# Two transformer blocks on one core: 64-row score products widened to 128 rows with zeros, and weight low parts moved from GpSimd to VectorE

## The chip, the cores and the metric

The kernel runs on one core of a Trainium2 chip. A core has five engines with instruction streams of their own: TensorE (PE; its weight loads are listed as PEld), VectorE (DVE), ScalarE (ACT), GpSimd (POOL) and SyncE (SP, which only issues transfers here). The metric is device time in microseconds; smaller is better.

## The reference, cut to what matters

A sequence of 512 tokens with 1024 features passes through four layers, all in float32: a latent attention (mla), a differential attention (diff), a convolution and pooling mixer, and a forgetting attention with a convolution. Each is followed by a layer norm, a SwiGLU feed-forward network (FFN) with 2816 hidden features and another layer norm. What the change touches:

```
# mla: 8 heads; a query and a key have a part of 128 features and a rotated part of 64
logits = einsum('bqhd,bkhd->bhqk', qn_b, k_nope) + einsum('bqhd,bkd->bhqk', qr_b, k_rope)
# diff: 8 heads with two maps (m) of 64 features each
logits = einsum('bqhmd,bkhmd->bmhqk', q_b, k) * scale - slopes * dist
p = softmax(where(chunk_mask, logits, NEG_BIG));  a = p[:, 0] - lam * p[:, 1]
# FFN
gate, up = split(x @ w_gu, 2);  y = (silu(gate) * up) @ w_down
```

## The kernel before, in words

**Precision.** A factor of a product is held as two float32r tiles, a high part (ScalarE copies, line 170 for weights) and a low part (the difference, line 171). `mm3` (lines 371 to 373) adds three products: high by high, low by high, high by low. A weight tile of 128x1024 is loaded by SP into `wraw` (2 buffers) and split into `whi` and `wlo` (5 buffers each). The tuple `ONPOOL` names the weights whose low part GpSimd makes; a list of exceptions turns single tiles around, none of them a `down` tile. The FFN's `win` tiles (gate and up together, combined by the sums of lines 193 to 198 as for a Strassen product) are always split by VectorE. Each of the four FFNs has 22 `down` tiles, the weights of its second product: 88 in all.

**First attention (mla).** Heads are worked in a pipeline: `scores(h + 1)`, `head(h + 2)`, `attend(h)`. A block of scores takes `mm3` over the 128 features, then line 981, where `sq` holds the rotated query's high part in rows 0 to 63 and its low part in rows 64 to 127 and `kk` holds the key's high part twice, and then line 982, the query's high part by the key's low part, over 64 rows only. There are 8 heads of 4 blocks, 128 to 512 columns wide.

**Second attention (diff).** The same pipeline. `stack` (line 1080) lays a query map's high and low part into the two halves of one 128-row tile, the other map the other way round, and duplicates the key's high part. Both maps' key low parts share one tile `kl`: map 0 in rows 0 to 63, map 1 in rows 64 to 127, with two buffers. A block is line 1164 (128 rows) and line 1166 (64 rows: high part of the query by `kl`), for each of two maps. The softmax is a VectorE reduction with a bias (line 1036), an exponential on ScalarE (1037) and, for diff, a combination of both maps on VectorE (1187); the result is transposed on PE (1052), split again (1065, 1067) and multiplied by the values in `attend`.

**Order.** Outside a few stretches written out by hand (in `project_out`), a scheduler in the build sets the order on every engine from the order of the code, the tiles' buffers and its own costs. At run time each engine works in that order and waits on semaphores. PSUM has four `acc`, two `ps` and two `tr` banks.

Of the kernel before, what the change touches and what calls it, by code (L numbers as in the profile page):

```python
# [10 lines left out]
F32R = mybir.dt.float32r  # L11
# [5 lines left out]
P = 128  # L17
S = 512
# [32 lines left out]

LNS = [(i, k) for s in ("", "_2") for i in range(2) for k in ("ln_mix_#" + s, "ln_ffn_#" + s)]

ONPOOL = ("od_x", "od_v", "od_q", "od_k", "od_o", "uq_n", "ukv", "df_o", "mla_o", "down")
OTHERWISE = (11, 12, 15, 20, 23, 24, 25, 73, 79, 80, 81, 82, 83, 84, 85, 86, 88, 90, 91, 100, 102, 103, 224, 226, 231)
NORM_ACT = (1, 3, 6, 7, 12, 13, 16, 24, 25, 26, 30)
ROPE_POOL = (1, 2, 3, 4, 5, 7, 9, 11)
# [18 lines left out]
HALF = (slice(0, 64), slice(64, 128))  # L76
# [66 lines left out]
class Weights:  # L143
# [30 lines left out]
    def steps(self):  # L174
# [7 lines left out]
        if name != "win":  # L182
            on_pool = (name in ONPOOL) != (self.at - 1 in OTHERWISE)
            self.ready.append((name, *self.split((self.hi, self.lo), raw[0], 0, n, nc.gpsimd if on_pool else nc.vector)))
# [129 lines left out]
def kernel(ctx: ExitStack, tc: tile.TileContext, a: dict, out: bass.AP):  # L314
    nc = tc.nc

    def f32(ap):
        return ap.bitcast(F32)
# [17 lines left out]
    def acc():  # L336
        return bank("acc")
# [496 lines left out]
    def mla(xT, close_x, open_x, names):  # L834
        with pool("mla_o") as op_:
            cmask = op_.tile([P, S], F32, name="cmask")
            with ExitStack() as st:
# [34 lines left out]
                for part, (key, n) in enumerate((("mla_a", 384), ("mla_b", 320))):  # L872
                    ps = [bank() for bank in ((acc,) * 4, (pss, pss, acc, acc))[part]]
# [11 lines left out]
                    for t in range(NT):  # L885
                        sq = ip.tile([P, 384], BF16, name="sq", tag="sq", bufs=2)
                        i = part * 4 + t
# [13 lines left out]
                kk = ap_.tile([P, S], F32R, name="kk")  # L901
                kkl = ap_.tile([P, S], F32R, name="kkl")

                QR = {}
                for u in range(2):
                    wh, wl = W.next("uq_r", 3, 256)
                    qr = ip.tile([P, NT, 4, 2, 64], F32, name="qr")
                    for t in range(NT):
                        ps = acc()
                        ts = slice(t * P, (t + 1) * P)  # L910
                        for k in range(3):
                            mm3(ps[:, :256], cqh[:, k, ts], cql[:, k, ts], wh[:, k], wl[:, k], k == 0, k == 2)
                        rope_on(qr[:, t], ps[:, :256].rearrange("p (h d) -> p h d", d=64), t, 4)
                    if u == 0:
                        for j in range(2):
                            turn_c(3 + j, ckh[:, j], ckl[:, j])
                        ps = pst()
                        for t in range(NT):
                            nc.tensor.transpose(ps[:, t * P:(t + 1) * P], kr[:, t].rearrange("p a b d -> p (a b d)"), ident)
                        nc.scalar.activation(kk, ps, AF.Copy)  # L920
                        nc.vector.tensor_sub(kkl[0:64], ps[0:64], f32(kk[0:64]))
                    for h in range(4):
                        ps = pst()
                        for t in range(NT):
                            nc.tensor.transpose(ps[:, t * P:(t + 1) * P], qr[:, t, h].rearrange("p a d -> p (a d)"), ident)
                        QR[4 * u + h] = sq = ap_.tile([P, S], F32R, name="sq_r", tag="sq_r", bufs=8)
                        nc.scalar.activation(sq, ps, AF.Copy, scale=-MLA_SCALE)
                        nc.vector.scalar_tensor_tensor(sq[64:128], ps[64:128], -MLA_SCALE, f32(sq[64:128]),
                                                       op0=OP.mult, op1=OP.subtract)
# [3 lines left out]
                Q, V, O = {}, {}, {}  # L933
# [37 lines left out]
                def scores(h):  # L971
                    qh, ql, kh, kl = Q.pop(h)
                    sq = QR.pop(h)
                    PT[h] = pt = Pt(cp, 2)
                    todo = []
                    for qb in range(NT):
                        n = (qb + 1) * P
                        qs = slice(qb * P, n)
                        ps = pss()
                        mm3(ps[:, :n], qh[:, qs], ql[:, qs], kh[:, :n], kl[:, :n], True, False)  # L980
                        nc.tensor.matmul(ps[:, :n], sq[:, qs], kk[:, :n], start=False, stop=False)
                        nc.tensor.matmul(ps[:, :n], sq[0:64, qs], kkl[0:64, :n], start=False, stop=True)
                        mark("mla", f"s{h}.{qb}")
                        e = cp.tile([P, S], F32, name="e", tag="e", bufs=2)
                        sums = small.tile([P, 4], F32, name="sums", tag="sums", bufs=6)
                        softmax(e, ps, n, cmask[:, S - n:], sums[:, 0:1], sums[:, 1:2])
                        todo.append((qb, n, e, sums))
                        if len(todo) > LAG:
                            rest(h, pt, *todo.pop(0))
                    while todo:  # L990
                        rest(h, pt, *todo.pop(0))
# [85 lines left out]
                mm3(ps[:, kb * P:], vh[kb], vl[kb], self.t[g, "h"][:, kb % 2, o:], self.t[g, "l"][:, kb % 2, o:],  # L1077
                    kb == 0, kb == NT - 1)

    def stack(p, ps, s, scale, i):  # L1080


        hi = [p.tile([P, S], F32R, name="qh", tag=f"qh{s}{m}", bufs=2) for m in range(2)]
        lo = [hi[m][HALF[1 - m]] for m in range(2)]
        if s:
            kl = p.tile([P, S], F32R, name="kl", tag="kl", bufs=2)
            lo = [kl[HALF[m]] for m in range(2)]
        for m in range(2):
            nc.scalar.activation(hi[m][HALF[m]], ps[HALF[m]], AF.Copy, scale=1.0 if s else scale)
        for m in range(2):  # L1090
            h = f32(hi[m][HALF[m]])
            if s:
                nc.vector.tensor_sub(lo[m], ps[HALF[m]], h)
                if i in DUP_ACT:
                    nc.scalar.activation(hi[m][HALF[1 - m]], h, AF.Copy)
                else:
                    nc.gpsimd.tensor_copy(hi[m][HALF[1 - m]], h)
            else:
                nc.vector.scalar_tensor_tensor(lo[m], ps[HALF[m]], scale, h, op0=OP.mult, op1=OP.subtract)
        return hi + [kl] if s else hi  # L1100

    def diff(xT, close_x, open_x, FIRST, names):
        with pool("df_o") as op_:
            st = ExitStack()
            dp = st.enter_context(pool("diff"))
# [14 lines left out]
            nc.vector.tensor_scalar(lam[:, 6:7], par("g_sub", 0), 1.0 - LAMBDA_INIT, None, op0=OP.mult)  # L1120
            nlam, gsub = lam[:, 5:6], lam[:, 6:7]
            xh, xl = xT
            Q, V, O = {}, {}, {}

            def values(p):
# [14 lines left out]
            def head(h):  # L1140
                got = []
                for s in range(2):
                    if h < 2:
                        ps = FIRST[2 * h + s]
                    else:
                        ps = acc()
                        project_T(ps, W.next(("df_q", "df_k")[s], KD, P), xT, KD)

                    got += stack(dp, ps, s, -0.125 * 2.0 ** (h + 1), h)
                Q[h] = got  # L1150

            PT, S0 = {}, {}

            def scores(h):
                q0, q1, k0, k1, kl = Q.pop(h)
                PT[h] = pt = Pt(dp, 2) if h < 7 else Pt(lp, 1)
                S0[h] = s0 = small.tile([P, 3, NT], F32, name="s0", tag="s0", bufs=3)
                todo = []
                for qb in range(NT):
                    n = (qb + 1) * P  # L1160
                    qs = slice(qb * P, n)
                    pm = [pss() for m in range(2)]
                    for m, (q, k) in enumerate(((q0, k0), (q1, k1))):
                        nc.tensor.matmul(pm[m][:, :n], q[:, qs], k[:, :n], start=True, stop=False)
                    for m, q in enumerate((q0, q1)):
                        nc.tensor.matmul(pm[m][:, :n], q[HALF[m], qs], kl[HALF[m], :n], start=False, stop=True)
                    mark("df", f"s{h}.{qb}")
                    sums = small.tile([P, 8], F32, name="sums8", tag="sums8", bufs=4)
                    e = []
                    for m in range(2):  # L1170
                        e.append(dp.tile([P, S], F32, name=f"e{m}", tag=f"e{m}", bufs=2))
                        softmax(e[m], pm[m], n, dist[:, S - n:], sums[:, m:m + 1],
                                s0[:, 0, qb:qb + 1] if m == 0 else sums[:, 2:3], 2.0 ** -(h + 1))
                    todo.append((qb, n, e, sums))
                    if len(todo) > LAG:
                        rest(pt, s0, *todo.pop(0))
                while todo:
                    rest(pt, s0, *todo.pop(0))
                nc.vector.reciprocal(s0[:, 1], s0[:, 0])
                nc.vector.tensor_mul(s0[:, 2], s0[:, 1], s0[:, 1])  # L1180
# [32 lines left out]
            def normalise(h, ps, ss):  # L1213
# [9 lines left out]
                O[h] = oh, ol  # L1223

            head(0)
            head(1)
            scores(0)
            values(0)
            late = None
            for h in range(8):  # L1230
# [544 lines left out]
    f = None  # L1775
    for step in steps:
        xT, f = step(xT, f)
# [108 lines left out]
```

## Time and profile before

| | |
|---|---|
| median of 3 runs | 2301.66 us (2300.28 to 2306.31) |
| the profiled execution | 2304.18 us, its span 2302.4 us |
| PE busy | 2250.3 us (98%), 14148 products |
| DVE busy | 1770.4 us (77%) |
| ACT busy | 997.1 us (43%) |
| POOL busy | 471.3 us (20%), 280 instructions |
| granted PE clock, mean | 0.989 |

The first attention's scores run from 64 to 173 us of the span and the second's from 588 to 792 us; the four FFNs lie around 200 to 560, 800 to 1190, 1300 to 1680 and 1910 to 2290 us. In the rows below a product's end is modelled and products overlap in the pipeline, so the distance from the start of one product to the start of the next is what it costs; the busy share alone does not show it.

### The profile page before, as it was taken

The page shows a single profiled execution, that of the slowest core. Times are in us where ns is not written, and L with a number is a line of the kernel's source. Part 1 is how long each engine was busy: PE and PEld are TensorE (multiplying, and loading weights), DVE is VectorE, ACT ScalarE, POOL GpSimd, SP SyncE. Part 2 cuts the span into 40 slices and gives each one's busy share as a digit, 9 for nine tenths or more (in the row PEclk, how much of TensorE's full clock was granted, in tenths as well). Part 3 has the DMA queues.
Part 4 walks back from the last instruction along what each step waited for, and adds up shares of the span by engine and source line. Part 5 has one row for each costly group of instructions (what it writes and reads, how often), then busy time and mean ns, then how long its engine had stood idle before and what let it go on. Part 6 is the DMA issues. An engine that isn't in the chain of part 4 may idle for free. (4 is left out here: it accounts for less than half of the span.)

```text
span 2302.4 us, 35345 instructions
## 1 busy us (share of the span) xinstructions
PE 2250.3 (98%) x14148; PEld 1988.6 (86%) x14148; DVE 1770.4 (77%) x2718; ACT 997.1 (43%) x1665; POOL 471.3 (20%) x280
## 2 busy tenths in 40 slices
PE   8999999999999999999999999999998999999997
PEld 8878999998888789999988899999886768999996
DVE  5667888886656688888765588888767766988886
ACT  4654444333555554443333244434334654444341
POOL 2200111113321111111210011111246531111112
PEclk9999999999999999999999999999998989999999
DMA  5112233332222033333233233332232112233321
GB/s 180 55 45 92 92 106 105 111 92 90 92 66 73 28 110 101 102 110 109 86 106 100 64 129 110 110 101 92 83 96 74 37 37 101 92 110 110 101 92 65
DMA packets 59365, 210.51 MB, mean 91 GB/s; under 512 B 6624, under 2 KB 6880, under 8 KB 59200
## 3 DMA queue, kind: packets, MB, share of 16 engines
q1 hardware_dynamic: 56304, 198.97, 27.5%
q0 software_dynamic: 2320, 8.23, 1.1%
q8 instruction: 111, 1.82, 0.3%
q10 hardware_dynamic: 576, 1.05, 0.1%
q14 instruction: 54, 0.44, 0.1%
HBM read 206.12 MB, written 2.10 MB: 90 GB/s over the span
## 5 line engine op out<-in xcount | busy, mean ns | idle before, releaser
L170 ACT ACTIVATE whi<-wraw 128x1024 fp32r<-128x1024 f32 (+3 forms) x528 | 521.0, 989 | 831.0 <-PE acc L372 301.3
L171 POOL TENSOR_TENSOR wlo<-wraw,whi 128x1024 fp32r<-128x1024 f32 (+2 forms) x141 | 355.8, 2526 | 1281.4 <-ACT whi L170 1030.2
L171 DVE TENSOR_TENSOR wlo<-wraw,whi 128x1024 fp32r<-128x1024 f32 (+3 forms) x387 | 429.3, 1110 | 136.8 <-ACT whi L170 136.1
L371 PE MATMUL acc<-xh,whi 128*128 128x256 f32 (+1 forms) x1712 | 527.3, 308 | 0.0
L372 PE MATMUL acc<-xl,whi 128*128 128x256 f32 (+1 forms) x1712 | 524.2, 306 | 3.1 <-DVE xl L481 3.1
L373 PE MATMUL acc<-xh,wlo 128*128 128x256 f32 (+1 forms) x1712 | 522.8, 305 | 3.1 <-DVE wlo L171 3.1
L372 PEld LDWEIGHTS acc<-xl,whi 128*128 128x128 f32 x1712 | 322.9, 189 | 28.5 <-DVE xl L481 4.3
L371 PEld LDWEIGHTS acc<-xh,whi 128*128 128x128 f32 x1712 | 322.9, 189 | 24.8 <-issue 0.9
L373 PE MATMUL acc<-xs,wlo 128*128 128x256 f32 x1216 | 342.6, 282 | 0.0
L372 PE MATMUL acc<-xql,whi 128*128 128x256 f32 x1216 | 341.4, 281 | 0.0
L371 PE MATMUL acc<-xs,whi 128*128 128x256 f32 x1216 | 340.0, 280 | 0.4 <-ACT sums L768 0.4
L373 PEld LDWEIGHTS acc<-xh,wlo 128*128 128x128 f32 x1712 | 322.9, 189 | 20.0 <-DVE wlo L171 4.1
L371 PEld LDWEIGHTS acc<-xs,whi 128*128 128x128 f32 x1216 | 229.9, 189 | 4.4 <-ACT sums L768 0.8
L372 PEld LDWEIGHTS acc<-xql,whi 128*128 128x128 f32 x1216 | 228.5, 188 | 5.7
L373 PEld LDWEIGHTS acc<-xs,wlo 128*128 128x128 f32 x1216 | 228.4, 188 | 0.0
L371 PE MATMUL tr<-whi,hh 128*128 128x512 f32 (+1 forms) x296 | 118.1, 399 | 0.0
L372 PE MATMUL tr<-wlo,hh 128*128 128x512 f32 (+1 forms) x296 | 116.9, 395 | 0.0
L373 PE MATMUL tr<-whi,hl 128*128 128x512 f32 (+1 forms) x296 | 115.8, 391 | 0.0
L373 PE MATMUL ps<-whi,hl 128*128 128x512 f32 x288 | 113.7, 395 | 0.0
L371 PE MATMUL ps<-whi,hh 128*128 128x512 f32 x288 | 113.2, 393 | 0.0
L372 PE MATMUL ps<-wlo,hh 128*128 128x512 f32 x288 | 113.2, 393 | 0.0
L431 DVE SCALAR_TENSOR_TENSOR res<-res,acc 128x512 f32<-128x512 f32 x87 | 58.9, 683 | 55.2 <-PE acc L373 54.9
(353 smaller groups left out, 4195.6 us busy)
## 6 DMA issues: line engine op xcount, KB each, us to landing
wraw<-in_gu_dram SPq DMA_DIRECT2D x176, 512.0 KB, 3.7
wraw<-in_dn_dram SPq DMA_DIRECT2D x88, 512.0 KB, 3.4
wraw<-in_ev_in_dram SPq DMA_DIRECT2D x16, 512.0 KB, 3.5
wraw<-in_mla_o_dram SPq DMA_DIRECT2D x8, 512.0 KB, 3.5
wraw<-in_df_q_dram SPq DMA_DIRECT2D x8, 512.0 KB, 3.4
wraw<-in_df_k_dram SPq DMA_DIRECT2D x8, 512.0 KB, 3.5
wraw<-in_df_v_dram SPq DMA_DIRECT2D x8, 512.0 KB, 3.4
wraw<-in_df_o_dram SPq DMA_DIRECT2D x8, 512.0 KB, 3.4
```

Of the source, the lines that this page charges most:

```text
L170: self.nc.scalar.activation(hi, raw[:, o:o + n], AF.Copy)
L171: eng.tensor_sub(lo, raw[:, o:o + n], hi.bitcast(F32))
L371: nc.tensor.matmul(ps, ah, bh, start=first, stop=False)
L372: nc.tensor.matmul(ps, ah, bl, start=False, stop=False)
L373: nc.tensor.matmul(ps, al, bh, start=False, stop=last)
L431: nc.vector.scalar_tensor_tensor(y, y, ALPHA if first else 1.0, ps, op0=OP.mult, op1=OP.add, accum_out=SUMS[t][:, c:c + 1] if sums else None)
```

## The change

Three edits. The key's low parts get tiles of their own, 128 rows high with zeros in the half that belongs to the other operand, and lines 982 and 1166 multiply over all 128 rows. In the second attention these are two tiles (`kl0`, `kl1`), made once for all heads, instead of one tile with two buffers; `scores(0)` now stands ahead of `head(1)`. And `down` leaves `ONPOOL`: its 88 low parts are made by VectorE.

```diff
-ONPOOL = ("od_x", "od_v", "od_q", "od_k", "od_o", "uq_n", "ukv", "df_o", "mla_o", "down")
+ONPOOL = ("od_x", "od_v", "od_q", "od_k", "od_o", "uq_n", "ukv", "df_o", "mla_o")
...
-                        nc.vector.tensor_sub(kkl[0:64], ps[0:64], f32(kk[0:64]))
+                        nc.vector.tensor_sub(kkl[HALF[0]], ps[HALF[0]], f32(kk[HALF[0]]))
+                        nc.gpsimd.memset(f32(kkl[HALF[1]]), 0.0)
...
-                        nc.tensor.matmul(ps[:, :n], sq[0:64, qs], kkl[0:64, :n], start=False, stop=True)
+                        nc.tensor.matmul(ps[:, :n], sq[:, qs], kkl[:, :n], start=False, stop=True)
...
-    def stack(p, ps, s, scale, i):
+    def keys_low(p):
+        kl = [p.tile([P, S], F32R, name=f"kl{m}") for m in range(2)]
+        for m in range(2):
+            nc.gpsimd.memset(f32(kl[m][HALF[1 - m]]), 0.0)
+        return kl
+
+    def stack(p, ps, s, scale, i, low=None):
...
-        lo = [hi[m][HALF[1 - m]] for m in range(2)]
-        if s:
-            kl = p.tile([P, S], F32R, name="kl", tag="kl", bufs=2)
-            lo = [kl[HALF[m]] for m in range(2)]
+        lo = [low[m][HALF[m]] if s else hi[m][HALF[1 - m]] for m in range(2)]
...
-                    for m, (q, k) in enumerate(((q0, k0), (q1, k1))):
+                    for m, (q, k, l) in enumerate(((q0, k0, l0), (q1, k1, l1))):
                         nc.tensor.matmul(pm[m][:, :n], q[:, qs], k[:, :n], start=True, stop=False)
-                    for m, q in enumerate((q0, q1)):
-                        nc.tensor.matmul(pm[m][:, :n], q[HALF[m], qs], kl[HALF[m], :n], start=False, stop=True)
+                        nc.tensor.matmul(pm[m][:, :n], q[:, qs], l[:, :n], start=False, stop=True)
...
             head(0)
+            scores(0)
             head(1)
-            scores(0)
             values(0)
```

Where instructions stand now. On PE, in the second attention, head 5's last score block (`ps_7500`, 512 columns) was followed by products of a projection (`acc_7916`) and head 6's first block (`ps_7787`), whose key low part has a buffer of its own (`kl_7616` beside `kl_7399`):

```order
L1164 MATMUL ps_7500<-qh_7397,qh_7360 128x512
L1166 MATMUL ps_7500<-kl_7399,qh_7360 128x512
L372 MATMUL acc_7916<-xl_5623,whi_7635 128x512
L373 MATMUL acc_7916<-xh_5622,wlo_7636 128x512
L1052 MATMUL tr_7516<-ident_76,e0_7474 128x128 x2
L371 MATMUL acc_7916<-xh_5622,whi_7635 128x512
L372 MATMUL acc_7916<-xl_5623,whi_7635 128x512
L373 MATMUL acc_7916<-xh_5622,wlo_7636 128x512
L1164 MATMUL ps_7787<-qh_7614,qh_7577 128x128
L1166 MATMUL ps_7787<-kl_7616,qh_7577 128x128
```

Now the same place reads so (`ps_7500` and `ps_7499` are head 5's last block, `ps_7785` head 6's first):

```order
L1170 MATMUL ps_7500<-qh_7398,qh_7361 128x512
L1171 MATMUL ps_7500<-kl1_6114,qh_7361 128x512
L1170 MATMUL ps_7499<-qh_7397,qh_7360 128x512
L1171 MATMUL ps_7499<-kl0_6113,qh_7360 128x512
L1053 MATMUL tr_7515<-ident_76,e0_7473 128x128 x2
L1170 MATMUL ps_7785<-qh_7613,qh_7576 128x128
L1171 MATMUL ps_7785<-kl0_6113,qh_7576 128x128
L371 MATMUL acc_7914<-xh_5623,whi_7633 128x512
```

Both heads use the one tile `kl0_6113`, with two transposes and one product between the last use by head 5 and the first by head 6; the projection's products stand behind. On DVE at that place, the write of the key low parts for head 6 (line 1098, 1093 before) now stands between the softmax reductions (line 1037) of the two maps of head 5's last block, and waits for PE:

```order
L1037 ISA e1_7509,sums8_7505<-ps_7500,dist_6101 128x512 [waits DVE_49,PE_49]
L1190 TENSOR_SCALAR sums8_7485<-sums8_7485,s0_7452,lam_6103 128x1 [waits DVE_49,Activation_49]
L1098 TENSOR_TENSOR kl0_6113<-acc_7582,qh_7613 64x512 [waits PE_49]
L1098 TENSOR_TENSOR kl1_6114<-acc_7582,qh_7614 64x512
L1037 ISA e0_7506,sums8_7505<-ps_7499,dist_6101 128x512 [waits PE_49]
L1104 SCALAR_TENSOR_TENSOR qh_7908<-acc_7877,qh_7908 64x512 [waits Activation_49]
```

Before, the same two writes (into `kl_7616`) stood about 45 instructions earlier on DVE and waited for ScalarE alone. In the first FFN, POOL's queue held one row of 23 low parts, 22 of them `down` tiles; now the one that is left is the next stage's:

```order
L419 DMA lnb<-in_ln_ffn_b_dram 128x1024
L171 TENSOR_TENSOR wlo<-wraw,whi 128x1024
L389 TENSOR_TENSOR lnr<-lnv,mhalf 128x1 x3
```

The 22 stand on DVE, among the sums of the `win` tiles (lines 193 to 198) and the additions that empty PSUM (771 to 782, 431). One hidden unit of the first FFN now, on DVE; the first row is a `down` tile:

```order
L171 TENSOR_TENSOR wlo<-wraw,whi 128x1024
L774 TENSOR_TENSOR sums<-sums,acc 128x256
L194 TENSOR_TENSOR wraw<-wraw 128x512
L777 TENSOR_TENSOR sums<-sums,acc 128x2x256
L431 SCALAR_TENSOR_TENSOR res_80<-res_80,ps 128x512
L197 TENSOR_TENSOR wraw<-wraw 128x512
L171 TENSOR_TENSOR wlo<-wraw,whi 128x1024
L198 TENSOR_TENSOR wraw<-wraw 128x512
L782 TENSOR_TENSOR sums<-sums,acc 128x512
```

## Rows read from the trace of the kernel before

**Rows 1.** The page's first part: busy us, share, instructions.

```profile
PE 2250.3 (98%) x14148; PEld 1988.6 (86%) x14148; DVE 1770.4 (77%) x2718; ACT 997.1 (43%) x1665; POOL 471.3 (20%) x280
```

**Rows 2.** Attention stretches: window, PE, PEld, DVE, ACT, POOL busy, PEclk, DMA, GB/s.

```profile
60.00:180.00 120.00, 118.61 (x630) 94.87 (x629) 78.90 (x218) 66.71 (x165) 16.33 (x8) 1.00 0.15 46
588.00:812.00 224.00, 220.32 (x1181) 176.14 (x1179) 139.86 (x383) 121.75 (x323) 50.23 (x31) 0.99 0.21 64
```

**Rows 3.** Sum over four FFN stretches: 260:540, 860:1140, 1350:1640, 1960:2240.

```profile
sum 1130.00, PE 1129.63 PEld 1048.02 DVE 971.77 ACT 457.81 POOL 193.99; mean PE 282.41 PEld 262.00 DVE 242.94 ACT 114.45 POOL 48.50
```

**Rows 4.** Lines 1166 and 982: count, ns min/median/max, starts, forms.

```profile
L1166 PE MATMUL ps<-kl,qh x64: 323/410/501, 588.8 to 791.8; 64*128 64x128 f32 x16, 64*128 64x256 f32 x16, 64*128 64x384 f32 x16, 64*128 64x512 f32 x16
L982 PE MATMUL ps<-kkl,sq_r x32: 323/410/502, 64.5 to 173.1; 64*128 64x128 f32 x8, 64*128 64x256 f32 x8, 64*128 64x384 f32 x8, 64*128 64x512 f32 x8
```

**Rows 5.** PE's timeline, a 512-column score block: start, us, line, tile.

```profile
685.41 0.39 PE L371 MATMUL acc<-xh,whi 128*128 128x512 f32 x1
685.64 0.39 PE L1164 MATMUL ps<-qh 128*128 128x512 f32 x1
685.95 0.50 PE L1166 MATMUL ps<-kl,qh 64*128 64x512 f32 x1
686.38 0.50 PE L372 MATMUL acc<-xl,whi 128*128 128x512 f32 x1
686.72 0.39 PE L373 MATMUL acc<-xh,wlo 128*128 128x512 f32 x1
```

**Rows 6.** PE's timeline, a 128-column score block behind products of values.

```profile
636.00 0.22 PE L371 MATMUL ps<-pth,vh 128*128 128x128 f32 x1
636.06 0.28 PE L372 MATMUL ps<-ptl,vh 128*128 128x128 f32 x1
636.18 0.27 PE L373 MATMUL ps<-pth,vl 128*128 128x128 f32 x1
636.29 0.28 PE L1164 MATMUL ps<-qh 128*128 128x128 f32 x1
636.49 0.32 PE L1166 MATMUL ps<-kl,qh 64*128 64x128 f32 x1
636.74 0.50 PE L371 MATMUL acc<-xh,whi 128*128 128x512 f32 x1
637.08 0.40 PE L372 MATMUL acc<-xl,whi 128*128 128x512 f32 x1
```

**Rows 7.** PE's timeline, two 64-row products side by side.

```profile
588.57 0.33 PE L1164 MATMUL ps<-qh 128*128 128x128 f32 x2
588.83 0.33 PE L1166 MATMUL ps<-kl,qh 64*128 64x128 f32 x2
589.09 0.38 PE L371 MATMUL acc<-whi,xh 128*128 128x256 f32 x1
589.31 0.28 PE L372 MATMUL acc<-wlo,xh 128*128 128x256 f32 x1
```

**Rows 8.** PE's waits: who waited for whom, total us, times, longest.

```profile
PE tr L1052 <- DVE e L1187: 1.6, 1, 1.6
PE ps L371 <- DVE sums L1036: 1.3, 2, 0.9
```

**Rows 9.** DVE by line and form: count | busy us, mean ns | idle before.

```profile
L171 DVE TENSOR_TENSOR wlo<-wraw,whi 128x1024 fp32r<-128x1024 f32 x299 | 366.3, 1225 | 114.4 <-ACT whi L170 114.2
L194 DVE TENSOR_TENSOR wraw<-wraw 128x512 f32<-128x512 f32 x76 | 99.8, 1313 | 0.0
L198 DVE TENSOR_TENSOR wraw<-wraw 128x512 f32<-128x512 f32 x76 | 91.8, 1207 | 0.1
L777 DVE TENSOR_TENSOR sums<-sums,acc 128x512 f32<-128x512 f32 x76 | 52.2, 687 | 3.8 <-PE acc L373 1.2
```

**Rows 10.** POOL's and DVE's timelines in the last FFN, at one `down` tile.

```profile
2241.44 2.54 POOL L171 TENSOR_TENSOR wlo<-wraw,whi 128x1024 fp32r<-128x1024 f32 x1 [13.11 <-ACT whi L170]
...
2241.75 2.79 DVE L197 TENSOR_TENSOR wraw<-wraw 128x512 f32<-128x512 f32 x1
```

More of the change, by code (lines that the diff above doesn't have):

```diff
@@ L1099, in stack @@
                 nc.vector.scalar_tensor_tensor(lo[m], ps[HALF[m]], scale, h, op0=OP.mult, op1=OP.subtract)
-        return hi + [kl] if s else hi
+        return hi + low if s else hi
     def diff(xT, close_x, open_x, FIRST, names):
@@ L1122, in diff @@
             xh, xl = xT
+            KL = keys_low(dp)
             Q, V, O = {}, {}, {}
@@ L1147, in head @@
                         project_T(ps, W.next(("df_q", "df_k")[s], KD, P), xT, KD)
-                    got += stack(dp, ps, s, -0.125 * 2.0 ** (h + 1), h)
+                    got += stack(dp, ps, s, -0.125 * 2.0 ** (h + 1), h, KL)
                 Q[h] = got
@@ L1154, in scores @@
             def scores(h):
-                q0, q1, k0, k1, kl = Q.pop(h)
+                q0, q1, k0, k1, l0, l1 = Q.pop(h)
                 PT[h] = pt = Pt(dp, 2) if h < 7 else Pt(lp, 1)
```

## The prediction

> **What bounds the kernel now.** The first view is the page's table of engines [rows 1]: PE is busy 98% of the span, the next one, DVE, 77%. That share alone says little, since the stages have different limits and a product's end is modelled. So the second view is the table of stretches. Over the four FFNs PE is busy 1129.63 of 1130 us, DVE 971.77 [rows 3]; in the first attention PE 118.61 of 120 and DVE 78.90, in the second 220.32 of 224 and 139.86 [rows 2]. PE sets the pace wherever the change reaches, at full granted clock (1.00, 1.00 and 0.99 in those rows), and an edit is worth what it takes out of PE's own sequence, less what PE then waits. The third view is PE's timeline, read from start to start [rows 5 to 7]: there the reader sees what the busy share hides, products that follow each other at a steady distance, and a stumble at each 64-row product.
>
> **The change part by part.** *64 rows to 128.* In a stream a 512-column product takes 0.23 us (685.41 to 685.64) and a 128-column one 0.06 (636.00 to 636.06). At the 512-column block the distances are 0.31 from line 1164 to the 64-row product, 0.43 from there to the next and 0.34 to the one after: 1.08 for three products that cost 3 x 0.23 = 0.69 in a stream, 0.39 more [rows 5]. At the 128-column block they are 0.20, 0.25 and 0.34: 0.79, where the stream takes 0.06 + 0.06 + 0.23 = 0.35, 0.44 more [rows 6]. That a group of sums ends there is not the reason: the 128-row product at 636.18 ends one too, and its successor follows after 0.11. So a 64-row product among 128-row ones costs about 0.39 us on top of its columns, at entry and at exit, and over 128 rows, zeros or not, it should cost the stream's distance. There are 32 in the first attention and 64 in the second, with the same durations in both [rows 4]. The first: 32 x 0.39 = 12.5. In the second, two pairs stand side by side; such a pair takes 0.74 from 588.57 to 589.31 with the product behind it, against 4 x 0.06 + 0.12 = 0.36 in a stream (256 columns at half of 512's), so 0.38 for two [rows 7]; 60 x 0.39 + 2 x 0.38 = 24.2. Together 36.7 us off PE. The bounds for this term are 0 (a 128-row product with zeros stumbles as well) and 36.7; I take the upper one, since the rows of 128-row products around it show no stumble anywhere.
>
> Rows 7 also show the other side: two products in different halves of the array run at the same time, one 0.33 us for both. Widened, they no longer can. The Trainium skill has both rules on one page (TensorEngine Tiling (Array Packing), Key Properties): changing the tiling mode drains the array, which speaks for the change, and different tiles execute in parallel, which speaks against it. By the second rule alone 32 products, one of each pair, were free before and would now be paid.
>
> *Zeros.* Three memsets go to POOL, which is busy 16.33 of 120 and 50.23 of 224 us in these stretches [rows 2]: nothing, and if POOL's idle time did not cover them, three of its mean instruction, 471.3 / 280 = 1.7, so 5 us [rows 1].
>
> *One pair of key tiles instead of two buffers.* At each of seven changes of head DVE's write of the new low part now waits for the last low product of the head before, and PE's first low product of the new head waits for DVE. The way round is that product, 0.50 (its own duration, row 685.95 of [rows 5]), and a 512-column DVE operation, 0.69 (nearest: line 777 in [rows 9]): 1.19, less what PE has in between. By the order, the early heads have a row of projection products there and the last changes little: two transposes and one product between heads 5 and 6. I take 1 us at each of the last three changes, 3 us; the bounds are 0 and 7 x 1.19 = 8.3. Behind the waiting write on DVE stand the reduction of the other map's block and the new head's query parts, and ScalarE's exponential waits for the first of these. The moved `scores(0)` costs nothing: PE has the 96 value products of 256 columns (96 x 0.12 = 11.5 us) to lay beside it.
>
> *The softmax behind a faster PE.* Scores go through DVE and ScalarE before PE turns them and multiplies by the values; those take as long as before, and PE now comes sooner, by 4 x 0.39 = 1.6 us a head in the first attention. Where PE waited for that chain already, the wait grows by this much. Three such waits show: two for line 1036 and one for line 1187, 1.3 and 1.6 us in total [rows 8]. I take 3 x 1.6 = 5 us; the bounds are 0 and the whole 36.7 (every head waits).
>
> *88 low parts to DVE.* They add 88 x 1.225 = 107.8 us to DVE [rows 9]. But POOL's work has a price on DVE now: at 2241.44 POOL starts a `down` tile for 2.54 us, and DVE's operation of 2241.75 takes 2.79 and ends with it [rows 10], where 512 columns take 0.69. In lines 194 and 198 alone this makes 76 x (1.313 - 0.687) + 76 x (1.207 - 0.687) = 87 us [rows 9]. So DVE's load in the FFNs should move by less than 107.8 - 87 = 21 us, on 971.77 of 1130. PE has nothing to gain there (0.37 us of idle time) and, while DVE keeps its 158 us of idle time, nothing to lose: 0. The cover is that idle time; what it costs if it is gone is the last rival. The end of the kernel, a chain on DVE behind the last products, is not touched.
>
> Sum: -36.7 + 0 + 3 + 5 + 0 = -28.7. From the profiled execution, 2304.18 us (span 2302.4 and 1.8 around it), this gives 2275.5. The median of the runs shown, 2301.66, lies 2.5 lower, so I forecast 2273.
>
> **The rivals.** *Nothing is late next.* The two waits stay away: 2301.7 - 36.7 = 2265. For it: the waits in rows 8 are few. Against: PE has 1.6 us a head less to cover a chain that was already late three times. 12 in 100.
>
> *The key tiles and the softmax take most of it.* All seven changes of head wait in full, 8.3, and six softmax waits grow instead of three, 6 x 1.6 = 9.6: a gain of 36.7 - 17.9 = 18.8, so 2301.7 - 18.8 = 2283; with nine, 2288. For it: the one pair of tiles ties PE and DVE together at each head. Against: the scheduler put products in between for the early heads. 14 in 100.
>
> *The change does not do what it says.* A 128-row product with zeros costs no less in its place: 2302. Or the parallel halves decide: with one product of each of the 32 pairs free before, 32 more at the mean of the four widths' distances (0.06 at 128, and 0.12, 0.17 and 0.23 as shares of 512's) make 32 x 0.145 = +4.6 us, 2306. Rows 7 show this at work, but only two pairs stand so, and the other 92 products are alone. 5 in 100 for both. The skill's second rule, named above, is this case.
>
> *Slower: DVE's queue holds up the FFNs.* DVE works in order, and the `down` low parts now stand in one queue with the `win` tiles that PE needs next and the additions that empty PSUM. If each comes late by its whole duration, PE idles 88 x 1.225 = 107.8 and the time is 2273 + 107.8 = 2381. DVE has 158 / 88 = 1.8 us of idle time per such tile today; the mechanism decides from where that falls short of 1.225 at the moment the tile is due, and the whole kernel is slower once about a third of the 88 come late so. Against it: even if no POOL stall went away, 971.77 + 107.8 is still 1080 of 1130. 2 in 100.
>
> **How the numbers follow.** The forecast's own case, 2266 to 2282, has 67 in 100. The range takes in the first rival's 2265 with some scatter and the second's 2283 and goes a little beyond: 2262 to 2286. About 0.3%, 7 us, is what a measurement of this kernel can tell from no change. Faster by more: the forecast and the first two rivals, 93. Within it: the third, 5. Slower: the last, 2.
>
> **What would show it.** Right: the distances around line 1171 (1166 before) and 983 (982) are those of the stream, 0.06 to 0.23; the attention stretches are shorter by some 9 to 10 and 18 to 20 us, the FFNs by none; DVE's 512-column operations of lines 194 and 198 fall to about 0.69; DVE's busy sum over the FFNs moves by less than 21 us. PE's new waits are for the key tiles, about 1 us at the last changes of head, and longer ones before the transposes and value products. Wrong: waits of PE for `wlo` in the FFNs, a 64-row stumble that stays at 128 rows, waits of several us at the changes of head, or a saving outside the attentions.

## The result, and the profile after

The changed kernel takes 2279.79 us in the median of 4 runs (2275.52 to 2284.52); the kernel before, run beside it, 2303.98 (2300.28 to 2310.22). The ratio is 0.9893, 95% interval 0.986 to 0.9925: 24.2 us less, against 28.7 in the prediction's sum. The profiled execution took 2284.52 us, its span is 2282.7.

The page's first part, the answer to [rows 1]: PE has lost 26.5 us of busy time, DVE 40.8 although it took over 88 operations, and POOL 224.7.

```profile
PE 2223.8 (97%) x14148; PEld 1987.0 (87%) x14148; DVE 1729.6 (76%) x2806; ACT 994.5 (44%) x1665; POOL 246.6 (11%) x195
```

Where the time went is read from landmarks that every version has. A stretch below runs from the last of the four squares of one layer norm (tile `junk`, line 449) to the last of the next norm's; the last FFN's runs to the end of the span. For the first attention, whose start hangs on the first loads, the distance from the first to the last product of the low keys `kkl` is taken. All in us, from one profiled execution each:

| | first attention | second attention | four FFNs, sum | scan stage |
|---|---|---|---|---|
| before | 108.6 | 266.9 | 1419.2 | 263.9 |
| changed kernel | 100.2 | 251.4 | 1419.6 | 267.3 |
| widening alone | 100.3 | 244.6 | 1420.4 | 261.1 |
| second attention's edits alone | 110.2 | 251.4 | 1420.2 | 258.5 |
| one key buffer | 100.2 | 252.8 | 1419.6 | 264.6 |
| two key buffers | 100.2 | 245.5 | 1419.5 | 261.2 |
| two key buffers, old order | 100.2 | 245.6 | 1419.6 | 258.3 |
| low parts made twice | 100.2 | 253.1 | 1450.4 | 261.6 |

The first attention gives 8.4 us, the second 15.5, the FFNs nothing. The scan stage is not touched by the change, and its length still moves by up to 9 us between versions. The granted clock moves it, as the columns of [rows 2] show in three pieces of that stage, first in the changed kernel, then in the one of the table's line "two key buffers, old order":

```profile
1820.00:1840.00 20.00, 19.04 (x96) 13.22 (x94) 15.35 (x35) 15.37 (x38) 9.84 (x6) 1.00 0.01 1
1840.00:1860.00 20.00, 19.51 (x57) 13.31 (x57) 8.72 (x23) 11.52 (x31) 6.48 (x4) 0.50 0.28 79
1860.00:1880.00 20.00, 17.30 (x86) 13.98 (x84) 12.86 (x24) 5.79 (x11) 3.44 (x2) 0.90 0.09 27
```

```profile
1820.00:1840.00 20.00, 18.23 (x83) 13.14 (x82) 12.29 (x31) 16.67 (x41) 8.94 (x5) 0.83 0.16 54
1840.00:1860.00 20.00, 17.27 (x82) 12.78 (x83) 12.18 (x22) 9.68 (x22) 4.76 (x2) 0.91 0.17 54
1860.00:1880.00 20.00, 20.00 (x98) 16.50 (x98) 12.83 (x24) 7.97 (x11) 5.80 (x3) 1.00 0.13 32
```

For the whole of one piece the changed kernel is at the lower of the two levels, 1.2 of 2.4 GHz, and gets 57 products done where the pieces around it hold 96 and 86; the other kernel is there for a part of two pieces only. So a few us in a median are this stage's, and the experiments are compared stage by stage. (The 110.2 us in the table's fourth line have this reason too: 0.98 granted there, 1.00 before.) The second attention is touched as well. These are the same columns for 10 us of it in the changed kernel, right behind PE's waits at a change of head, and for the same 10 us in the widening alone:

```profile
720.00:730.00 10.00, 8.37 (x28) 6.09 (x29) 7.49 (x20) 3.73 (x9) 0.00 (x0) 0.83 0.16 53
720.00:730.00 10.00, 8.05 (x44) 6.67 (x42) 7.86 (x18) 6.83 (x16) 2.85 (x2) 1.00 0.15 52
```

At 0.83, PE can lose 1.7 of 10 us. One such piece stands in the second attention of the kernel before (0.83 from 750 to 760 us), of the changed kernel, of the second attention's edits alone and of both lines with two key buffers, none in the widening alone, and 0.66 in one such piece of the line with one key buffer. So differences between these stretches hold up to 1.7 us of the clock, with one key buffer 3.4.

PE's timeline in the second attention of the changed kernel (start, us, engine, line, form), a 512-column low product (line 1171, 1166 before) as in [rows 5], and a 128-column one as in [rows 6]:

```profile
591.52 0.28 PE L372 MATMUL acc<-wlo,xh 128*128 128x256 f32 x1
591.63 0.40 PE L1170 MATMUL ps<-qh 128*128 128x512 f32 x1
591.87 0.39 PE L1171 MATMUL ps<-kl,qh 128*128 128x512 f32 x1
592.10 0.28 PE L373 MATMUL acc<-whi,xl 128*128 128x256 f32 x1
592.22 0.28 PE L371 MATMUL acc<-whi,xh 128*128 128x256 f32 x1
...
597.07 0.39 PE L371 MATMUL acc<-xh,whi 128*128 128x512 f32 x1
597.30 0.22 PE L1171 MATMUL ps<-kl,qh 128*128 128x128 f32 x1
597.36 0.45 PE L372 MATMUL acc<-xl,whi 128*128 128x512 f32 x1
597.65 0.40 PE L373 MATMUL acc<-xh,wlo 128*128 128x512 f32 x1
```

The starts are 0.24, 0.23 and 0.12 apart at the first, 0.23, 0.06 and 0.29 at the second. The entry into the low product and the product itself have no stumble left; behind the 128-column one the next product comes 0.06 late, as it does behind products of values: in [rows 6] a 128-column product behind another of its kind takes 0.12 and 0.11, and 0.06 only behind a wider one.

DVE by line and form, the answer to [rows 9]: 88 more of line 171, and lines 194 and 198 at the price of line 777.

```profile
L171 DVE TENSOR_TENSOR wlo<-wraw,whi 128x1024 fp32r<-128x1024 f32 x387 | 473.9, 1225 | 88.8 <-ACT whi L170 87.9
L777 DVE TENSOR_TENSOR sums<-sums,acc 128x512 f32<-128x512 f32 x76 | 52.1, 686 | 2.1
L194 DVE TENSOR_TENSOR wraw<-wraw 128x512 f32<-128x512 f32 x76 | 52.0, 685 | 0.2
L198 DVE TENSOR_TENSOR wraw<-wraw 128x512 f32<-128x512 f32 x76 | 51.9, 682 | 0.1
```

The sum over four FFN stretches of the same lengths less 3 us in all (252:532, 838:1117, 1328:1617, 1939:2218), the answer to [rows 3]:

```profile
sum 1127.00, PE 1127.00 PEld 1046.40 DVE 932.15 ACT 458.96 POOL 2.39; mean PE 281.75 PEld 261.60 DVE 233.04 ACT 114.74 POOL 0.60
```

And PE's waits in the second attention (who waited for whom, total us, times, longest), the answer to [rows 8]:

```profile
PE ps L1170 <- DVE sums L1037: 2.9, 4, 1.0
PE tr L1207 <- DVE ptl L1068: 1.2, 1, 1.2
PE ps L1171 <- DVE kl L1098: 0.9, 2, 0.5
...
PE acc L371 <- DVE kl L1098: 0.8, 2, 0.4
```

The long wait for line 1187 is gone and shorter ones have come, four of them named after the key tile `kl`. Here is the change from head 5 to 6 that they belong to, from the timeline of all engines (in brackets the idle time before an instruction, and who ended it; lines between are left out):

```profile
720.29 0.40 PE L1171 MATMUL ps<-kl,qh 128*128 128x512 f32 x1
...
720.73 1.20 ACT L1094 ACTIVATE qh<-acc 64x512 fp32r<-64x512 f32 x2
720.94 0.28 DVE L1068 TENSOR_TENSOR ptl<-tr,pth 128x128 fp32r<-128x128 f32 x1
721.14 0.68 DVE L1037 CUSTOM_DVE_ANT_0 e<-ps,dist 128x512 f32<-128x512 f32 x1
721.17 0.41 PE L1053 MATMUL tr<-ident,e 128*128 128x128 f32 x2 [0.48 <-DVE ol L382]
...
721.88 0.33 PE L1170 MATMUL ps<-qh 128*128 128x128 f32 x1 [0.30 <-DVE sums L1037]
721.93 1.40 DVE L1098 TENSOR_TENSOR kl<-acc,qh 64x512 fp32r<-64x512 f32 x2
...
722.66 0.33 PE L1171 MATMUL ps<-kl,qh 128*128 128x128 f32 x1 [0.45 <-DVE kl L1098]
...
723.36 0.69 DVE L1037 CUSTOM_DVE_ANT_0 e<-ps,dist 128x512 f32<-128x512 f32 x1
723.38 0.50 PE L371 MATMUL acc<-xh,whi 128*128 128x512 f32 x1 [0.40 <-DVE kl L1098]
```

The last low product of the old head starts at 720.29. The new key parts come after it: 1.20 us of ScalarE's copies, and at 721.93, with these and what stood in DVE's queue done, 1.40 of DVE's two writes. PE gets two short steps in between, and the softmax of the next block starts behind the writes at 723.36. PE's waits for `kl` and for the softmax stand around two changes of head: 2.7 us between 719 and 723.4, and 2.9 us between 741 and 749.6.

### The profile page after: what moved, and what is told of

The parts are those of the page before. It is cut to its first block, busy times and chain, and to the rows that moved or that the text cites. A ratio compares the mean times of both kernels' runs of the same rounds, so it can differ in the third digit from the quotient of the medians.

```text
span 2282.7 us, 35239 instructions
## 1 busy us (share of the span) xinstructions
PE 2223.8 (97%) x14148; PEld 1987.0 (87%) x14148; DVE 1729.6 (76%) x2806; ACT 994.5 (44%) x1665; POOL 246.6 (11%) x195
## 5 line engine op out<-in xcount | busy, mean ns | idle before, releaser
L171 DVE TENSOR_TENSOR wlo<-wraw,whi 128x1024 fp32r<-128x1024 f32 (+2 forms) x475 | 536.8, 1131 | 117.0 <-ACT whi L170 116.0
L171 POOL TENSOR_TENSOR wlo<-wraw,whi 128x1024 fp32r<-128x1024 f32 (+2 forms) x53 | 130.4, 2463 | 548.0 <-ACT whi L170 547.6
L389 POOL TENSOR_TENSOR lnr<-lnv,mhalf 128x1 f32<-128x1 f32 x32 | 23.7, 740 | 1264.4 <-DVE lnv L387 1264.4
L782 DVE TENSOR_TENSOR sums<-sums,acc 128x512 f32<-128x512 f32 x76 | 52.2, 687 | 85.5 <-PE acc L373 85.0
```

Source lines behind the costliest of these rows:

```text
L171: eng.tensor_sub(lo, raw[:, o:o + n], hi.bitcast(F32))
L389: nc.gpsimd.tensor_tensor(r[:, :n], v[:, :n], mhalf[:, :n], op=OP.pow)
L782: nc.vector.tensor_add(g[:, 1:3], g[:, 1:3], v)
```

## The experiments

Each kernel differs from the kernel before or from the changed one by the edit shown. Ratios are to the kernel before, run beside it.

**The widening alone.** The shared tile of low parts, in its two buffers, is simply read over 128 rows; in the first attention its other half gets a copy of the same low parts from the operation that was there.

```diff
-  nc.vector.tensor_sub(kkl[0:64], ps[0:64], f32(kk[0:64]))
+  nc.vector.tensor_sub(kkl, ps, f32(kk))
-  nc.tensor.matmul(ps[:, :n], sq[0:64, qs], kkl[0:64, :n], start=False, stop=True)
+  nc.tensor.matmul(ps[:, :n], sq[:, qs], kkl[:, :n], start=False, stop=True)
-  nc.tensor.matmul(pm[m][:, :n], q[HALF[m], qs], kl[HALF[m], :n], start=False, stop=True)
+  nc.tensor.matmul(pm[m][:, :n], q[:, qs], kl[:, :n], start=False, stop=True)
```

> The kernel before with the 96 low-key products over 128 rows and nothing else moved: no zeros and no pair of key tiles (the other half of the tile holds the other map's low part, in the first attention a copy of the same one, so each product also adds low part times low part), every engine's instructions in the order of the kernel before. Stumble theory, with the give-back due to the one pair of key tiles and the order that comes with it: the first attention is shorter by 7 to 10 us, the second by 20 to 24, since both key buffers are there; in all 27 to 34 us. Rival 1, the give-back is the softmax chain, which is late behind a faster PE whatever the key tiles are: the second attention is shorter by about 15.5 us, as in the changed kernel, and the total by 20 to 24. Rival 2, the gain comes from the new order and not from the rows: both stages stay within 2 us of before.

Measured: 2271.16 us, ratio 0.9867 (0.9849 to 0.9886); first attention 8.3 shorter, second 22.3. VectorE, ScalarE and GpSimd work in the order of before, and so does PE but for one product at 581 us that stands two places earlier, so the 30.6 us belong to the row count, less what the clock had in them: the second attention of before has a piece at 0.83, this one has none, which is up to 1.7 us. (With two key buffers and one such piece on both sides the second attention is 21.3 us shorter than before.) The second rival (the order) is out, and the first (a softmax that takes 9 us whatever the keys are) too: without the pair of key tiles the second attention is 6.8 us shorter than in the changed kernel, of which at most 1.7 is the clock. PE's longest waits there now, in the columns of [rows 8]:

```profile
PE tr L1052 <- DVE e L1187: 2.1, 1, 2.1
PE acc L371 <- ACT oh L381: 0.8, 1, 0.8
PE ps L1164 <- DVE sums L1036: 0.6, 1, 0.6
```

It is the wait for line 1187 of before, 0.5 longer, and none for `kl`.

**The three parts of the change, each alone.** The first attention's edits, the second attention's edits with the order, and `"down"` out of `ONPOOL`, each put into the kernel before as the diff has them.

> The kernel before with only the first attention's edits of the change (32 products over 128 rows, the zeros on POOL). Theory: the first attention is shorter by the 7.6 us that the changed kernel shows, the rest within 1 us except for the scan stage, whose length moves by some us with the clock; total -7 to -8. Rival, the zeros or the moved order cost something there: the widening alone (the run beside it) gains 2 us or more over this one in the first attention.

> The kernel before with only the second attention's edits (64 products over 128 rows, one pair of key tiles with zeros, scores(0) ahead of head(1)); the FFN low parts stay on POOL. Theory: the second attention is shorter by about 15.5 us as in the changed kernel, with PE waits of some 9 us in the changes of head after the fifth, the other stages as before; total -15 to -16. Rival, the low parts moved to DVE feed into the second attention: it comes out different from 15.5 by 3 us or more.

> The kernel before with the 88 low parts on DVE and nothing else. Theory, DVE has the room: the FFNs stay at their length within 1 us each, total 0 within 3 us; DVE's busy time falls by about 40 us over the kernel, since its 512-column operations no longer run beside POOL's and go back to 0.69 us. Rival, DVE's queue holds PE up: longer by up to 108 us. Rival, POOL's tiles had held PE up: shorter by several us in the FFNs.

Measured: 2296.80 us, ratio 0.9972 (0.996 to 0.9985); 2287.15, 0.9939 (0.9921 to 0.9957); 2303.92, 1.0002 (0.9988 to 1.0016). In us of 2303.4 that is -6.4, -14.1 and +0.5, together -20.0 where the whole change has -24.2 with an interval of about 8 either way: they add up within what is measured. The first attention is 100.3 us from first to last low product both with the zeros and without them, so the zeros cost nothing. With the second attention's edits alone that attention takes the 251.4 us of the changed kernel. The low parts on DVE alone leave the FFNs at 1419.3 us against 1419.2, and DVE's busy time falls from 1770.4 to 1730.4 us, as expected.

**Two key buffers, in the new order and in the old.** The changed kernel with the shared tile in two buffers, read over 128 rows, in place of the pair; then also `scores(0)` behind `head(1)` again.

```diff
-  KL = keys_low(dp)
-  lo = [low[m][HALF[m]] if s else hi[m][HALF[1 - m]] for m in range(2)]
+  low = [p.tile([P, S], F32R, name="kl", tag="kl", bufs=2)] * 2 if s else None
+  lo = [low[m][HALF[m]] if s else hi[m][HALF[1 - m]] for m in range(2)]
```

> The changed kernel with the pair of key tiles replaced by one tile in two buffers that holds the low parts of both maps and is read over all 128 rows (so each product also adds low part times low part); scores(0) stays ahead of head(1), the low parts of the FFN stay on DVE. Theory, the single pair is what gave back about 7 us: the stretch of the second attention, from the norm before it to the norm behind it, falls from the 251.4 us of the changed kernel to about 244.6, and PE's waits at 717 to 755 us go; total -6 to -7 against the changed kernel. Rival, the moved scores(0) gave it back: the stretch stays at 250 to 252.

> As the run with two key buffers, with scores(0) behind head(1) again, as in the kernel before. Theory (the single pair): within 1 us of the run with two key buffers in the second attention. Rival (the moved scores(0)): 6 to 7 us shorter than that run.

Measured: 2276.50 us, ratio 0.9877 (0.9857 to 0.9897), and 2269.69, 0.9854 (0.9832 to 0.9876). The second attention takes 245.5 and 245.6 us, with one piece at 0.83 each as in the changed kernel: the pair gives back 5.9 us and the moved `scores(0)` nothing. In the whole the first of the two is only 3.3 us below the changed kernel's 2279.79, where 6 to 7 were expected, and 6.8 above the second; their intervals overlap. The clock parts the two medians: its mean over a run is 0.987 to 0.990 in the first one's runs and 0.991 to 0.994 in the second's, and the scan stage, where most of it is lost, takes 261.2 against 258.3 us in the profiles.

**One buffer of the shared tile.** The widening alone, with `bufs=1` for `kl`.

> The widening alone (the tile of low parts that both maps share, read over 128 rows) with one buffer of that tile instead of two. Theory, the single buffering is the cost of the changed kernel's pair: the stretch of the second attention goes from 244.6 us back to about 251, PE waits for the key tile or for what is queued behind its write, 0.4 to 1.4 us each, at the changes of head after the fifth; total +6 to +7 against the widening alone. Rival, it was the pair itself (two tiles, zeros, lows written apart): the stretch stays within 1.5 us of 244.6.

Measured: 2278.57 us, ratio 0.9892 (0.9874 to 0.991), the second attention 252.8 us: 8.2 more than with two buffers, of which up to 3.4 is the lower clock there. So the buffer count by itself costs about what the pair costs, and two tiles, zeros and separate writes need play no part. PE's first waits there:

```profile
PE ps L1166 <- DVE kl L1093: 2.4, 2, 1.2
PE ps L1164 <- DVE sums L1036: 2.3, 3, 0.9
PE tr L1052 <- DVE ol L382: 1.5, 2, 1.2
```

**The widening with the low parts on DVE.** Both edits above in the order of the kernel before.

> The widening alone, in the order of the kernel before, and the 88 low parts on DVE. Theory, the low parts are worth nothing: within 2 us of the 2271.2 of the widening alone, stage by stage. Rival, freeing POOL and the stalled DVE operations shortens some stage now that PE is faster: 2 us or more below it.

Measured: 2274.77 us, ratio 0.9869 (0.9847 to 0.989); 244.5 us in the second attention, 1419.1 in the FFNs, and 264.6 in the scan stage. Outside that stage it is 1.2 us below the widening alone (2273.0 - 264.6 = 2008.4 against 2270.7 - 261.1 = 2009.6). The low parts are worth about 1 us at most, and a single profile of each does not tell that from nothing.

**Low parts made twice.** In the changed kernel each `down` low part on DVE is made two times in a row; in a second version the repeat is written over the raw weights instead.

```diff
   eng.tensor_sub(lo, raw[:, o:o + n], hi.bitcast(F32))
+  if twice:
+      eng.tensor_sub(lo, raw[:, o:o + n], hi.bitcast(F32))    # second version: into raw[:, o:o + n]
```

> The changed kernel with each of the low parts of the second FFN product's weights that are on DVE made twice in a row there (88 more operations of 1.225 us, 108 us of DVE work). Theory, DVE's idle time covers the low parts: DVE had 932 of 1127 us of load in the FFN stretches, so 1040 of 1127 still fits and the total moves by 0 to 10 us. Rival, DVE's queue: PE waits for what stands behind each second operation, 1.2 us each, up to 108 us longer.

> The changed kernel with a second operation of the same size behind each low part of the second FFN product's weights on DVE, as in the run that made them twice, but written over the raw weights, which nobody waits for except the next load, and not over the tile that PE waits for. That run was 27 us slower than the changed kernel. Theory, PE waited there because the tile it needs was finished one operation later: here the cost is less than half, 0 to 12 us. Rival, the room on DVE's queue was used up, whoever waits for the second operation: again 25 us or more.

Measured: 2310.10 us, ratio 1.0031 (1.0014 to 1.0049), and 2317.60, 1.0065 (1.0045 to 1.0085). The FFNs are 30.8 us longer than in the changed kernel, and 37.0 in the second version (1456.6). The theory missed twice, and in the second run the rival's figure was the right one: the cost does not hang on who reads what the repeat writes. Of 88 x 1.225 = 108 us put on DVE, about a third shows; a few us of this are clock, which falls behind PE's waits (0.77 from 525 to 540 us in the first version, 1.00 at the end of that FFN in the changed kernel). Yet DVE is busy for 963.35 of 1127 us in the first version:

```profile
sum 1127.00, PE 1117.87 PEld 1032.12 DVE 963.35 ACT 442.72 POOL 0.00; mean PE 279.47 PEld 258.03 DVE 240.84 ACT 110.68 POOL 0.00
```

PE's waits for low parts, in the changed kernel, the first version (its line 376 is line 373) and the second:

```profile
PE acc L373 <- DVE wlo L171: 2.9, 5, 0.8
```

```profile
PE acc L376 <- DVE wlo L171: 13.4, 9, 2.6
...
PE ps L375 <- DVE wlo L173: 5.1, 12, 1.4
```

```profile
PE acc L376 <- DVE wlo L171: 25.0, 24, 3.4
```

DVE's idle 164 us are not where the low parts are due. Whether the queue alone does this is open: both repeats also read the raw weights, and so keep one of their two buffers longer. ScalarE's waits for the loads of `win` grow, in the changed kernel, the first version and the second:

```profile
ACT whi L170 <- DMA wraw<-in_gu_dram: 102.4, 101, 4.0
ACT whi L170 <- DMA wraw<-in_gu_dram: 267.0, 146, 4.3
ACT whi L170 <- DMA wraw<-in_gu_dram: 257.3, 146, 3.6
```

In the kernel before, the same wait is 208.8 us, with PE idle for 0.37 us in the four stretches of [rows 3], which speaks for the queue; no run separates the two.

**Pairs of 64-row products.** The kernel before with the two low products of a block issued one right behind the other in a section of their own, over 64 rows in different halves, and the same frame with 128 rows.

```diff
+  with tc.tile_critical():
       for m, q in enumerate((q0, q1)):
           nc.tensor.matmul(pm[m][:, :n], q[HALF[m], qs], kl[HALF[m], :n], start=False, stop=True)
           # second kernel: q[:, qs], kl[:, :n]
```

> The kernel before with the two 64-row products of each block of the second attention issued directly one behind the other (32 such pairs; a section of its own on PE, whose branches cost some time, which the next run has too). Theory, the stumble is paid at the change between 128 and 64 rows: a pair costs about 0.38 us more than its two widened products in the next run, 32 x 0.38 = 12 us in the second attention. Rival 1, the stumble belongs to each 64-row product: 64 x 0.39 = 25 us more than the next run. Rival 2, the halves run at the same time and this decides: 32 x 0.145 = 4.6 us less than the next run.

> The run above with the two products over 128 rows, in the same frame and the same order. Theory: 12 us shorter than that run in the second attention; rival 1: 25 us shorter; rival 2: 4.6 us longer. Against the widening alone it is longer by what the frame's branches cost.

Measured: 2355.95 us, ratio 1.0231 (1.0209 to 1.0252), and 2360.76, 1.025 (1.0223 to 1.0276). The second attention takes 316.8 and 320.0 us: 64 rows are 3.2 us shorter, near the second rival and the opposite of the theory; this is one profile of each, and the intervals of the ratios overlap. The timelines show a pair in its surroundings, 64 rows first:

```profile
642.96 0.40 PE L372 MATMUL acc<-xl,whi 128*128 128x512 f32 x1
643.79 0.44 PE L1167 MATMUL ps<-kl,qh 64*128 64x384 f32 x2 [0.43 <-issue]
644.32 0.49 PE L373 MATMUL acc<-xh,wlo 128*128 128x512 f32 x1
644.65 0.40 PE L371 MATMUL acc<-xh,whi 128*128 128x512 f32 x1
```

```profile
599.06 0.28 PE L373 MATMUL acc<-whi,xl 128*128 128x256 f32 x1
599.79 0.50 PE L1167 MATMUL ps<-kl,qh 128*128 128x256 f32 x2 [0.46 <-issue]
600.38 0.38 PE L371 MATMUL acc<-whi,xh 128*128 128x256 f32 x1
```

In this frame PE stands empty ahead of every pair, for 0.43 to 2.1 us and 29.6 us in all; the granted clock in the stage is 0.91 and 0.92. Both are a large part of the 70 us by which the stage is too long, and the empty PE takes away what was to be measured, the change between row counts in a running stream. What is left shows the halves at work together (the distances from a pair's start to the next product sum to 24.3 us with 64 rows and 29.9 with 128): the second product of a 64-row pair starts 3 ns behind the first in the median of every width, that of a 128-row pair 164 to 464 ns. So the pairs in a stream stay untested; for them there is only the one in [rows 7].

## Why the prediction was right, and where not

**64 rows to 128: right, 36.7 forecast, 32.2 measured over 93 of the 96 products.** With the order held fixed, the distances around the low products exceed the stream's by 12.3 us in the first attention and 24.2 in the second before (31 and 62 products, those without a wait, each distance counted once), and by 1.9 and 2.5 in the widening alone. That is 10.4 + 21.8. The 0.39 us per product is about right for 256 columns and more. For the 24 products of 128 columns it is 0.28 to 0.30 by PE's timelines, because the price of the stream was misread: [rows 6] has 0.12 and 0.11 for 128 columns behind 128, where I put 0.06, and the timeline above has 0.29 for 512 columns behind 128, where I put 0.23. So the stream takes 0.11 + 0.11 + 0.29 = 0.51 there, and that block's excess was 0.79 - 0.51 = 0.28 and not 0.44. Most of what remains over 128 rows, 0.14 to 0.16 per product, stands at these. In the second attention nine low products also follow the one before at a distance of two products; the step between is one, and the sum of 0.39 each counts it twice. The rule of the Trainium skill that a change of tiling mode drains the array (TensorEngine Tiling (Array Packing), Key Properties) fits the 0.39 us lost by a 64-row product and its absence over 128 rows; a drain itself no trace shows. The other on the same page, that different tiles run in parallel, agrees with the 3 ns above.

**Zeros: right, 0.** The first attention is the same with and without them.

**One pair of key tiles: the step that failed, 3 forecast, 5.9 measured** with the same clock on both sides (6.8 against the widening alone, 8.2 for one buffer of the shared tile, both with some clock in them). Its place was right, the late changes of head, though two and not three; its price was not. The way round was put at 0.50 + 0.69 = 1.19. The timeline above has 3.0 us from the old head's last low product to the end of the key writes: ScalarE's copies of 1.20 come first, DVE writes two halves and not one, and both engines have other work in their queues. And a wait for `kl` is only part of it; the next block's softmax stands behind the writes, as the prediction said of the queue without giving it a price.

**Softmax behind a faster PE: 5 forecast, about 3 left over, the cause in part argued.** In the widening alone the first attention gets 8.3 of 10.4 us; the second gets 22.3 with up to 1.7 of clock in it, of 21.8. So 2.1 and about 1 are given back. The waits bear out a part: PE's listed waits in the first attention grow from 1.3 to 2.3 us, 0.5 of it before a transpose of the softmax's result, and in the second the wait for line 1187 grows by 0.5. For the rest no run names the cause.

**88 low parts to DVE: right, 0.** The FFNs moved by 0.4 us. DVE's busy sum was to move by less than 21 us and fell by 39.6, over stretches 3 us shorter: next to lines 194 (47.8 us less) and 198 (39.9), which the sum had, line 197 lost 21.1, the low parts `hl` of line 379 15.7, and line 717 10.2. With POOL's tiles gone all have their own price again. In [rows 10] DVE's operation does not end with POOL's, as the prediction has it, but 0.56 us behind it (2244.54 and 2243.98), near its own price. The Trainium skill says that a DVE operation with two SBUF inputs and a GpSimd operation that reads SBUF shut each other out of a shared port for a whole instruction (SBUF — State Buffer, "SBUF: two separate sides"); the trace agrees: 2.79 us in [rows 10], 0.69 now.

**The sum.** -32.2 + 5.9 + 3 is about -23; the two attentions are 23.9 us shorter in the profiles, and -24.2 was timed, with an interval of about 8 either way. This checks little, since the softmax's 3 is what the other terms leave. Against the forecast of -28.7 the widening brought 4.5 less and the key tiles cost 2.9 more, and the softmax took about 2 less; that the last has the other sign helped the number. The signs named for the stages were missed too: 8.4 us in the first attention where 9 to 10 were expected, 15.5 in the second for 18 to 20. Of the 6.8 us between 2279.8 and the forecast's 2273, 2.3 is the kernel before, 2303.98 here against 2301.66. In the profiled executions alone the difference is 19.7, since the scan stage took 3.4 us more at its lower clock.

**The rivals.** "Nothing late next" (2265) and "most is taken" (2283) both had a part of it; 2279.8 lies between the second and the forecast. The slower one, more work on DVE, does cost time, from a point further out than these 88 tiles and short of twice as many; that it is the queue and not the raw buffers held longer is not shown. The argument against it, 1080 of 1130 us, was too weak: at 963 of 1127 it already cost 31.

## What to carry to other kernels

Here a product over half the rows, alone among products over all rows, was not cheaper: it paid 0.39 us on top of its columns; fill the other half, with zeros or with whatever is harmless there. Before buffers are given up for such zeros, look whether the other half of the operand may hold something real: here the other map's low parts, times low parts of the queries, would do, and kept both buffers. The version with the shared tile, two buffers and the order of before took 2269.69 us, 0.9854 of before, and is the lowest of those run; from the widening alone, 2271.16, it cannot be told apart. And, as far as the low parts made twice show, idle time of an engine in a mean covers an added operation only where that idle time falls ahead of what is due.

## What the hardware showed that was not expected

- A 64-row product in a stream of 128-row ones costs 0.39 to 0.40 us more than the stream (12.3 us for 31, 24.2 for 62), more than the 0.23 of a whole 512-column product.
- A 128-column product takes 0.06 us from start to start behind a wider one and 0.11 behind another of 128 columns, and a 512-column one behind it 0.29 in place of 0.23.
- Two 64-row products in different halves, issued behind an empty PE, start 3 ns apart; 128-row ones start 164 to 464 ns apart.
- An added DVE load of 108 us makes the FFNs 31 to 37 us longer while DVE still shows 164 us of idle time; the raw weights are held longer too.
